# Attention's v product with seven block products from left sums in seven of its sixteen units, and v between k and q in two head groups

## The chip, the cores and the metric

One core of one Trainium2 chip runs the kernel, and one launch computes the whole network. The time is device microseconds of one execution; the median of three runs before the change is 2031.22 us (2029.69 to 2031.56). Engines are named as in the profile: PE (TensorE), ACT (ScalarE), DVE (VectorE), POOL (GpSimd) and SP (the engine that issues most DMAs).

## The reference: what is computed

A decoder of two layers on one sequence of 256 tokens with 2048 features, all in float32. Layer 0 is a pooling mixer and a gated FFN with a causal convolution of width 3; layer 1 is attention and another such FFN. What matters here is the attention:

```python
k_shared = (h @ shared_w_k).reshape(B_, S, N_HEADS, HEAD_DIM)
v_shared = (h @ shared_w_v).reshape(B_, S, N_HEADS, HEAD_DIM)
q = (h @ w_q).reshape(B_, S, N_HEADS, HEAD_DIM)
...
s = jnp.where(mask, s, NEG_INF)
m = jnp.max(s, axis=-1, keepdims=True)
pr = jnp.exp(s - m)
...
o = jnp.sum(wts[..., None] * jnp.stack(outs, axis=0), axis=0)
return o.reshape(B_, S, D_MODEL).astype(h.dtype) @ w_o
```

There are 16 heads of 128 features. With 256 tokens the three dilated branches come down to one softmax with a table of counts (`cnt`) and one of masks (`negm`).

## The kernel before

**Units.** The program is a list of units, and each unit multiplies one block of a weight matrix (512 rows by 512 columns) with the activations. `run_units` (L126) goes through the list: `ahead` (L111) issues the loads of the blocks up to five units ahead and splits the blocks up to three units ahead, then the unit's matmuls follow, then the pieces of work that `later(n, ...)` has put n units off, and last the evacuation of a group that is complete. A raw block has one of three buffers, a split block one of four.

**Split.** Every float32 operand is made of a high part and a low part (`wh` and `wl`, type fp32r). For a plain block ACT rounds the high part (L82) and DVE subtracts it (L83). A product of two such operands takes three matmuls: high by high, high by low, low by high.

**Two kinds of product.** `group` (L177) gives the result with features on the partitions. A pair there is one matmul of 512 columns, which does both halves of x at once (L165), and one of 256 (L166); a unit has 16 pairs. k and q are made in this way. `group_tm` (L189) gives it with tokens on the partitions: in `go_t` a unit is 24 matmuls of 512 columns (L238 to L240). All sixteen v units are of this kind before the change. `group_tm` has a second form, `mk_seven` (L202), used until now in the FFN's down projection alone. It treats tokens by features by columns as a product of 2 by 2 blocks and takes seven block products for eight (Strassen's scheme in Winograd's order), so that a unit has 7 x 2 x 3 = 42 matmuls of 256 columns (L227 to L229). It comes as two entries of the list, here called the a half (three products, 18 matmuls) and the b half (four products, 24 matmuls). Its block is split by `split_sums` (L90): for the a half ACT runs L103 twice and DVE L104, L106 twice, L107 and L109, for the b half ACT runs L96 twice and DVE L97 twice. It needs four sums of blocks of the left operand, each in high and low part.

**Attention.** The heads come in four head groups of four heads; they are numbered 0 to 3 here. Before the change each group runs four k units, four q units and four v units. What follows a group's q is put off by units: `scores` of heads 0 and 1 after two units and of heads 2 and 3 after three (PE L988 and L989, then a softmax of small steps on DVE and ACT, L994 to L1011). In groups 0 to 2 the probabilities are turned without PE: `blocks` (L1030) lets DVE transpose blocks of 32 by 32 for two heads at once (L1034, tile `pb`), and 16 DMAs on SP then move the blocks to their places (`move`, L1040 to L1043, tile `pTs`). This is done for heads 0 and 1 four units after q and for heads 2 and 3 seven units after q; the DMAs go in two lots of eight, one and two units later. Tile `pb` has one buffer, so the second transposition waits until the first 16 moves have landed. `outputs` (L1048) multiplies with v: heads 0 and 1 four units after v, heads 2 and 3 seven units after v (PE L1056 and L1057, then ACT L1058 and DVE L1059).

Each engine runs its own instructions in a fixed order, SP its DMAs too; an instruction whose inputs or buffers are not there yet holds up all that stand behind it on its engine.

## Time and profile before

| what | value |
|---|---|
| median of three runs (range) | 2031.22 us (2029.69 to 2031.56) |
| the profiled execution | 2031.27 us; its span 2029.5 us, 1.8 us lie around it |
| busy share: PE, weight load, DVE, ACT | 100%, 89%, 82%, 62% |
| chain that ended last | PE 99% |
| from head group 0's q to the end of head group 3's v | 953.1 to 1219.2 us of the span |
| granted PE clock over the span | 0.999 |

Times in the trace are microseconds from the span's start. "Busy" of PE counts a matmul from its start to a modelled end, and matmuls overlap in the pipeline: a matmul of 512 columns is shown with about 396 ns and one of 256 with about 281 ns. What a unit costs is therefore read from the distance between the starts of two units, not from these durations.

### The profile page before, as it was taken

To read this page: it belongs to the slowest core of one execution; us is meant where nothing else is said; L and a number is where in the kernel's file an instruction comes from. 1 tells how busy PE (TensorE), PEld (TensorE's weight loads), DVE (VectorE), ACT (ScalarE), POOL (GpSimd) and SP (SyncE) were. 2 spreads that over 40 slices of the span, in tenths; PEclk is the share of its full clock that TensorE was granted. 3 is DMA by queue.
4 is the path that set the end of the run, shared out by engine and by line. 5 is a ranking of instruction groups with operands and counts; after the bars stand their busy time and mean duration, and the time that the engine had idled before them with its cause. 6 is when DMAs were issued, how large, how long until landed. Compare 5 with 4: busy or idle time off the path is not lost.

```text
span 2029.5 us, 31025 instructions
## 1 busy us (share of the span) xinstructions
PE 2021.9 (100%) x12460; PEld 1807.1 (89%) x12460; DVE 1664.9 (82%) x1979; ACT 1253.3 (62%) x1676; POOL 75.0 (4%) x111
## 2 busy tenths in 40 slices
PE   9999999999999999999999999999999999999999
PEld 8898988899889988889888888998899989989987
DVE  6859887899789988879756657787889888989898
ACT  6544686667766675657533444577667676667672
POOL 2000000000000001100000000000000000100100
PEclk9999999999999999999999999999999999999999
DMA  8565467666655667864566555557666756666665
GB/s 258 203 206 189 164 208 208 192 191 227 207 193 188 229 206 206 229 221 166 193 197 192 169 185 171 187 177 218 187 197 198 228 187 212 198 214 197 208 213 180
DMA packets 278304, 405.90 MB, mean 200 GB/s; under 512 B 80414, under 2 KB 95668, under 8 KB 277904
## 3 DMA queue, kind: packets, MB, share of 16 engines
q1 hardware_dynamic: 266144, 389.72, 58.0%
q0 software_dynamic: 11584, 13.55, 4.4%
q8 instruction: 97, 1.59, 0.3%
q10 hardware_dynamic: 432, 0.66, 0.1%
q14 instruction: 47, 0.39, 0.1%
HBM read 380.01 MB, written 2.10 MB: 188 GB/s over the span
## 4 chain that ended last, share of the span: by engine, by line
PE 99%; DMA 0%; SPq 0%; DVE 0%; ACT 0%; issue 0%; DVEq 0%
PE acc L165 43%; PE acc L166 22%; PE t L238 3%; PE t L240 3%; PE t L239 3%; PE acc L169 3%; PE acc L170 3%; PE acc L168 3%; PE s L228 3%; PE s L227 2%; PE s L229 2%; PE t L228 2%; PE t L227 2%; PE t L229 2%; PE s L989 0%; PE o L1056 0%
## 5 line engine op out<-in xcount | busy, mean ns | idle before, releaser
L165 PE MATMUL acc<-xc,wh 128*128 128x512 f32 x3264 | 1151.9, 396 | 0.0
L166 PE MATMUL acc<-xc,wl 128*128 128x256 f32 x3264 | 915.9, 281 | 0.0
L83 DVE TENSOR_TENSOR wl<-raw,wh 128x2048 fp32r<-128x2048 f32 (+2 forms) x322 | 697.0, 2169 | 251.7 <-ACT wh L82 248.6
L165 PEld LDWEIGHTS acc<-xc,wh 128*128 128x128 f32 x3264 | 615.9, 189 | 144.0 <-DVE o L1059 0.6
L82 ACT CAST wh<-raw 128x2048 fp32r<-128x2048 f32 (+2 forms) x322 | 582.0, 1812 | 221.4 <-PE acc L165 120.3
L166 PEld LDWEIGHTS acc<-xc,wl 128*128 128x128 f32 x3264 | 615.4, 189 | 0.5
L96 ACT CAST wh<-raw 128x1024 fp32r<-128x1024 f32 x108 | 112.9, 1053 | 149.0 <-DVE raw L107 123.1
L97 DVE TENSOR_TENSOR wl<-raw,wh 128x1024 fp32r<-128x1024 f32 x108 | 129.1, 1221 | 1.4 <-ACT wh L96 1.4
L103 ACT CAST wh<-raw 128x1024 fp32r<-128x1024 f32 x108 | 84.5, 832 | 48.5 <-PE acc L165 33.8
L586 ACT ACTIVATE c<-u,cv 128x256 f32<-128x256 f32 x172 | 89.6, 594 | 18.7 <-DVE f L649 8.2
L106 DVE TENSOR_TENSOR wl<-raw,wh 128x1024 fp32r<-128x1024 f32 x108 | 98.3, 951 | 1.7 <-ACT wh L103 1.4
L228 PE MATMUL t<-wl,g 128*128 128x256 f32 x320 | 89.8, 281 | 0.0
L227 PE MATMUL t<-wh,g 128*128 128x256 f32 x320 | 89.8, 281 | 0.0
L229 PE MATMUL t<-wh,g 128*128 128x256 f32 x320 | 89.7, 280 | 0.0
L271 POOL DMA_DIRECT2D ht<-w x24 | 20.3, 847 | 1809.2 <-ACT wh L103 771.9
L577 ACT COPY u<-acc 128x256 f32<-128x256 f32 x164 | 54.7, 373 | 51.5 <-PE acc L166 51.4
L591 ACT ACTIVATE a<-u,cv 128x256 f32<-128x256 f32 x172 | 73.5, 500 | 12.3 <-DVE g L659 6.5
L229 PE MATMUL s<-wh,xs 128*128 128x256 f32 x284 | 79.2, 279 | 0.0
L228 PE MATMUL s<-wl,xs 128*128 128x256 f32 x284 | 79.2, 279 | 0.0
L227 PE MATMUL s<-wh,xs 128*128 128x256 f32 x284 | 79.2, 279 | 0.0
L591 ACT ACTIVATE u<-u,cv 128x256 f32<-128x256 f32 x172 | 73.5, 500 | 0.0
L238 PE MATMUL t<-wh,g 128*128 128x512 f32 (+1 forms) x179 | 68.2, 381 | 0.0
(279 smaller groups left out, 3439.2 us busy)
## 6 DMA issues: line engine op xcount, KB each, us to landing
raw<-in_ffn_w_up_dram SPq DMA_DIRECT2D x160, 1024.0 KB, 4.9
raw<-in_ffn_w_down_dram SPq DMA_DIRECT2D x80, 1024.0 KB, 5.1
raw<-in_pool_w_out_dram SPq DMA_DIRECT2D x16, 1024.0 KB, 5.0
raw<-in_shared_w_k_dram SPq DMA_DIRECT2D x16, 1024.0 KB, 5.0
raw<-in_attn_w_q_dram SPq DMA_DIRECT2D x16, 1024.0 KB, 5.3
raw<-in_shared_w_v_dram SPq DMA_DIRECT2D x16, 1024.0 KB, 5.9
raw<-in_attn_w_o_dram SPq DMA_DIRECT2D x16, 1024.0 KB, 5.0
raw<-in_pool_w_in_dram SPq DMA_DIRECT2D x12, 1024.0 KB, 5.4
```

The source lines that it names most:

```text
L82: A.copy(wh[i][:, s], r[:, s])
L83: V.tensor_tensor(wl[i][:, s], r[:, s], wh[i][:, s].bitcast(F32), OP.subtract)
L96: A.copy(h[:, :, n], r[:, :, n])
L97: V.tensor_tensor(l[:, :, n], r[:, :, n], h[:, :, n].bitcast(F32), OP.subtract)
L106: V.tensor_tensor(l[:, k, n], r[:, k, n], h[:, k, n].bitcast(F32), OP.subtract)
L165: PE.matmul(ps[m], h[:, k, c], q[:, k, :, :T], start=st, stop=False)
L166: PE.matmul(ps[m][:, :T], l[:, k, c], q[:, k, 0, :T], start=False, stop=sp and not shifted)
L227: PE.matmul(to, xh, h[:, k, n], start=opens and kk == 0, stop=False)
L228: PE.matmul(to, xh, l[:, k, n], start=False, stop=False)
L229: PE.matmul(to, xl, h[:, k, n], start=False, stop=ends and kk == 1)
L238: PE.matmul(to, xh, h[:, k, c], start=j == 0 and k == 0, stop=False)
L591: A.activation(to[:, m, :], u[:, m, i:i + T], AF.Copy, scale=cv[:, i, j:j + 1])
```

## The change

Seven of the sixteen v units take the form of `mk_seven`: in head groups 1 and 2 the blocks 1, 2 and 3 of the rows, in head group 3 block 3. In head groups 1 and 2 the v units now stand between the k units and the q units. The left sums of x are formed once, by `v_sums` (DVE additions on 128x256, then a split on ACT and DVE), four units after the q of head group 0; those of block 3 take five small tiles, those of blocks 1 and 2 one tile `xsum` each. v is evacuated by `v_early` (ACT copies, DVE adds; four of the products) and by additions in `v_post`, where a copy stood before. `outputs` of groups 0 to 2 are now put off from q instead of v, by eight and eleven units; `transposes` and `outputs` of group 3 are as before. An a half and a b half count as one unit each in these distances.

Of k, v and q in the head groups 1 and 2 the list now reads: four k units, one plain v unit, a and b halves of three v units, four q units. Lines move: scores L988 is now L1044, `blocks` L1034 is L1090, the moves L1043 are L1099, `outputs` L1056 and L1057 are L1112 and L1113, its copies L1059 are L1115, the evacuation of q and k L974 is L1026.

PE at the outputs of heads 0 and 1 of head group 1. In the kernel before they stand between the fourth k unit and the first q unit of head group 2 (each `wh` number is one weight block; `acc` is the result of k, then of q):

```order
L165 MATMUL acc<-xc,wh_10267 128x512
L166 MATMUL acc<-xc,wl_10268 128x256
L1056 MATMUL o<-pTs,vt 128x256
L1057 MATMUL o<-pTs,vt 128x128
L1056 MATMUL o<-pTs,vt 128x256
L1057 MATMUL o<-pTs,vt 128x128
L165 MATMUL acc<-xc,wh_10317 128x512
L166 MATMUL acc<-xc,wl_10318 128x256
```

In the changed kernel they stand between the a half and the b half of the second seven-product unit of head group 2's v (`t` and `s` are banks of the v product, `xsum` the left sums):

```order
L229 MATMUL t_10573<-wh_10564,xsum 128x256
L1112 MATMUL o<-pTs,vt 128x256
L1113 MATMUL o<-pTs,vt 128x128
L1112 MATMUL o<-pTs,vt 128x256
L1113 MATMUL o<-pTs,vt 128x128
L227 MATMUL s_10576<-wh_10609,xsum 128x256
L228 MATMUL s_10576<-wl_10610,xsum 128x256
```

In both kernels the fourth k unit and the transposition of heads 0 and 1 lie before these rows; what PE has between the transposition and the outputs was four units of k and is now one plain v unit, one a half, one b half and one a half. The outputs of heads 2 and 3 now follow the third b half.

DVE from the first transposition (`pb<-p`) of head group 1 to the second. Before the change:

```order
L83 TENSOR_TENSOR wl_10232<-raw_10107,wh_10231 128x2048
L1034 STREAM_TRANSPOSE pb<-p 128x768
L952 COPY vt<-t_10082 128x512
L83 TENSOR_TENSOR wl_10268<-raw_10168,wh_10267 128x2048
L83 TENSOR_TENSOR wl_10318<-raw_10229,wh_10317 128x2048
L83 TENSOR_TENSOR wl_10364<-raw_10265,wh_10363 128x2048
L1034 STREAM_TRANSPOSE pb<-p 128x768
```

In the changed kernel (`k<-k,acc` is the evacuation of k; two seven-product blocks, `raw_10438` and `raw_10562`, are split between the transpositions):

```order
L97 TENSOR_TENSOR wl_10513<-raw_10329,wh_10512 128x4x256 x2
L1090 STREAM_TRANSPOSE pb<-p 128x768
L1026 TENSOR_TENSOR k<-k,acc 128x256 x4
L104 TENSOR_TENSOR raw_10438<-raw_10438 128x2x256
L106 TENSOR_TENSOR wl_10565<-raw_10438,wh_10564 128x4x256
L106 TENSOR_TENSOR wl_10565<-raw_10438,wh_10564 128x2x256
L107 TENSOR_TENSOR raw_10438<-raw_10438 128x2x256
L109 TENSOR_TENSOR raw_10438<-raw_10438 128x4x256
L97 TENSOR_TENSOR wl_10610<-raw_10438,wh_10609 128x4x256 x2
...
L109 TENSOR_TENSOR raw_10562<-raw_10562 128x4x256
L1090 STREAM_TRANSPOSE pb<-p 128x768
L97 TENSOR_TENSOR wl_10682<-raw_10562,wh_10681 128x4x256 x2
```

The scores' steps and one seven-product split (a half, then b half) stand ahead of the first transposition here, where plain splits stood.

SP's queue at the same place in the changed kernel (`raw` is a load of a weight block, `pTs<-pb` a move):

```order
L72 DMA raw_10562<-in_shared_w_v_dram 128x4x512
L1099 DMA pTs<-pb 32x6x32 x16
L72 DMA raw_10641<-in_attn_w_q_dram 128x4x512
L72 DMA raw_10679<-in_attn_w_q_dram 128x4x512
L1099 DMA pTs<-pb 32x6x32 x8
L72 DMA raw_10724<-in_attn_w_q_dram 128x4x512
L1099 DMA pTs<-pb 32x6x32 x8
```

Before the change a load stood between the first eight moves and the second eight; now the sixteen follow each other, and the second sixteen have a load in their middle as before.

The diff:

```diff
--- before.py
+++ after.py
@@ -943,19 +943,71 @@
     scale = 1.0 / math.sqrt(P)
     qk, pr, oq, pT, vts = {}, {}, {}, {}, {}
 
+    def v_tile(c):
+        if c not in vts:
+            vts[c] = pools["attn"].tile([P, 2, 512], F32, name="vt", tag="vt")
+        return vts[c][:, 0, :], vts[c][:, 1, :]
+
     def v_post(c):
         def post(t, ps):
-            if t == 0:
-                vts[c] = pools["attn"].tile([P, 2, 512], F32, name="vt", tag="vt")
-                A.copy(vts[c][:, 0, :], ps)
+            v = v_tile(c)[t]
+            if c > 0:
+                V.tensor_tensor(v, v, ps, OP.add)
+            elif t == 0:
+                A.copy(v, ps)
             else:
-                V.tensor_copy(vts[c][:, 1, :], ps)
-                if c == 3:
-                    later(1, lambda: transposes(c, (0, 1)))
-                    later(2, lambda: transposes(c, (2, 3)))
-                later(2 if c == 3 else 4, lambda: outputs(c, (0, 1)))
-                later(3 if c == 3 else 7, lambda: outputs(c, (2, 3)))
+                V.tensor_copy(v, ps)
+            if t == 1 and c == 3:
+                later(1, lambda: transposes(c, (0, 1)))
+                later(2, lambda: transposes(c, (2, 3)))
+                later(2, lambda: outputs(c, (0, 1)))
+                later(3, lambda: outputs(c, (2, 3)))
         return post
+
+    def v_early(c):
+        def early(p16, p75):
+            v0, v1 = v_tile(c)
+            left, right = v0[:, :256], v0[:, 256:]
+            A.copy(left, p16[:, :256])
+            V.tensor_tensor(right, left, p16[:, 256:], OP.add)
+            V.tensor_tensor(v1[:, :256], right, p75[:, :256], OP.add)
+            V.tensor_tensor(right, right, p75[:, 256:], OP.add)
+            V.tensor_tensor(v1[:, 256:], v1[:, :256], p75[:, 256:], OP.add)
+        return early
+
+    vsums = {}
+
+    def v_sums(q, then):
+        ap = pools["attn"]
+        x = H[q]
+        a11, a12, a21, a22 = (x[:, k:k + 2, t * P:t * P + P] for k, t in ((0, 0), (2, 0), (0, 1), (2, 1)))
+        f = ap.tile([P, 4, T], F32, name="f", tag="k")
+        d = [f[:, i].rearrange("p (k t) -> p k t", k=2) for i in range(4)]
+        V.tensor_tensor(d[0], a21, a22, OP.add)
+        V.tensor_tensor(d[1], d[0], a11, OP.subtract)
+        V.tensor_tensor(d[2], a21, a11, OP.subtract)
+        V.tensor_tensor(d[3], a12, d[1], OP.subtract)
+
+        def rest():
+            if q < 3:
+                t = quad_tile("xsum")
+                vsums[q] = [[t[:, i, hl, :T].rearrange("p (k t) -> p k t", k=2) for hl in range(2)] for i in range(4)]
+                split_act(t, f)
+                then()
+                return
+            w = lnp.tile([P, 2, T], F32R, name="vs0", tag="fold2")
+            z = ap.tile([P, 2, T], F32R, name="vs3", tag="vs3")
+            vs = [[w[:, 0], w[:, 1]], [z[:, 0], z[:, 1]]]
+            for pair in (("S", "Q"), ("cs", "f1")):
+                vs.append([lnp.tile([P, T], F32R, name=f"vs{nm}", tag=nm) for nm in pair])
+            for i, v in enumerate(vs):
+                A.copy(v[0], f[:, i])
+            for i, v in enumerate(vs):
+                V.tensor_tensor(v[1], f[:, i], v[0].bitcast(F32), OP.subtract)
+            vsums[q] = [[u.rearrange("p (k t) -> p k t", k=2) for u in v] for v in vs]
+            then()
+
+        later(1, rest)
 
     def qk_post(nm, hq):
         def post(ps):
@@ -978,6 +1030,10 @@
                 if hq < 3:
                     later(4, lambda: blocks(hq, (0, 1)))
                     later(7, lambda: blocks(hq, (2, 3)))
+                    later(8, lambda: outputs(hq, (0, 1)))
+                    later(11, lambda: outputs(hq, (2, 3)))
+                if hq == 0:
+                    later(4, lambda: v_sums(3, lambda: v_sums(1, lambda: v_sums(2, lambda: None))))
         return post
 
     def scores(hq, ms):
@@ -1058,11 +1114,20 @@
             A.copy(oq[hq][:, m, 0, :T], ps[:, :T])
             V.tensor_tensor(oq[hq][:, m, 1, :T], ps[:, :T], oq[hq][:, m, 0, :T].bitcast(F32), OP.subtract)
 
+    def v_group(hq):
+        js = (0, 1, 2, 3)
+        seven = {0: (), 1: (1, 2, 3), 2: (1, 2, 3), 3: (3,)}[hq]
+        group_tm(shared_w_v, rows4, 512 * hq, 512, xsrcs, v_post(hq),
+                 seven={j: (lambda j=j: vsums[j]) for j in js if j in seven}, early=v_early(hq))
+
     for hq in range(4):
         x0 = hq == 0
         group(shared_w_k, rows4, 512 * hq, 512, psrcs if x0 else xsrcs, qk_post("k", hq), mode="x" if x0 else "ab")
+        if hq in (1, 2):
+            v_group(hq)
         group(attn_w_q[0], rows4, 512 * hq, 512, xsrcs, qk_post("q", hq))
-        group_tm(shared_w_v, rows4, 512 * hq, 512, xsrcs, v_post(hq))
+        if hq in (0, 3):
+            v_group(hq)
     add_last(attn_w_o[0], rows4, [lambda j=j: oq[j] for j in range(4)], True, 1, 0, after=to_tokens)
     marks.append(len(units))
     ffn(1)
```

## The prediction

> **What bounds the kernel now.** I read the page first: the shares of the engines, then the chain that ended last.
>
> ```profile
> PE 2021.9 (100%) x12460; PEld 1807.1 (89%) x12460; DVE 1664.9 (82%) x1979; ACT 1253.3 (62%) x1676; POOL 75.0 (4%) x111
> PE 99%; DMA 0%; SPq 0%; DVE 0%; ACT 0%; issue 0%; DVEq 0%
> ```
>
> PE never rests and makes up 99% of the chain, so a matmul less is time less, as long as nothing makes PE wait; and each wait that the change brings to PE is lost in full. Two questions follow: what seven products save per unit, and whether the cover of everything that runs beside v is still there.
>
> Next, the stages by windows. The rows are: two plain v units of head group 1 (48 matmuls; the counts include those that reach over an edge), two seven-product units of the FFN (84 matmuls), four k units, one pair of outputs, and the whole of group 1's v with both pairs of scores.
>
> ```profile
> 1048.70:1059.85 11.15, 11.15 (x51) 9.02 (x49) 5.03 (x4) 4.09 (x3) 0.00 (x0) 1.00 0.54 190
> 1841.35:1851.27 9.92, 9.92 (x86) 9.92 (x85) 8.60 (x12) 9.66 (x14) 0.00 (x0) 1.00 0.35 120
> 1073.64:1096.16 22.52, 22.52 (x129) 19.65 (x128) 13.85 (x9) 8.04 (x6) 0.00 (x0) 1.00 0.66 197
> 1096.16:1097.39 1.23, 1.23 (x11) 1.13 (x9) 0.00 (x0) 0.37 (x1) 0.00 (x0) 1.00 1.21 260
> 1048.70:1073.64 24.94, 24.94 (x114) 20.45 (x113) 17.41 (x49) 10.90 (x14) 0.00 (x0) 1.00 0.49 169
> ```
>
> A plain v unit takes 11.15 / 2 = 5.58 us, a seven-product unit 9.92 / 2 = 4.96, a k or q unit 22.52 / 4 = 5.63, a pair of outputs 1.23, both pairs of scores 24.94 - 4 x 5.58 = 2.64. Of the 4.96 the a half has 18 of 42 matmuls, 2.13 us, the b half 2.83.
>
> **The change: what PE saves.** Seven units go from 5.58 to 4.96: 7 x 0.62 = **-4.3 us**. The rows of the order leave no doubt that the matmuls go away.
>
> **What DVE gets.** The rows by form, for a plain block and then for the pieces of a seven-product block:
>
> ```profile
> L83 DVE TENSOR_TENSOR wl<-raw,wh 128x2048 fp32r<-128x2048 f32 x282 | 645.0, 2289 | 238.2 <-ACT wh L82 235.3 <-DMA pTs<-pb 2.0 <-PE vT L1128 0.4
> L97 DVE TENSOR_TENSOR wl<-raw,wh 128x1024 fp32r<-128x1024 f32 x108 | 129.1, 1221 | 1.4 <-ACT wh L96 1.4
> L109 DVE TENSOR_TENSOR raw<-raw 128x1024 f32<-128x1024 f32 x54 | 66.2, 1225 | 1.8
> L106 DVE TENSOR_TENSOR wl<-raw,wh 128x1024 fp32r<-128x1024 f32 x54 | 65.8, 1219 | 1.7 <-ACT wh L103 1.4
> L107 DVE TENSOR_TENSOR raw<-raw 128x512 f32<-128x512 f32 x54 | 37.4, 692 | 1.9
> L104 DVE TENSOR_TENSOR raw<-raw 128x512 f32<-128x512 f32 x54 | 36.9, 684 | 0.0
> L106 DVE TENSOR_TENSOR wl<-raw,wh 128x512 fp32r<-128x512 f32 x54 | 36.9, 683 | 0.0
> ```
>
> The a half costs DVE 0.68 + 1.22 + 0.68 + 0.69 + 1.23 = 4.50 us and the b half 2 x 1.22 = 2.44, so 6.94 against 2.29 for a plain block, and against 4.96 on PE. Alone this is no wait: splits run three units ahead. But it moves what stands behind them on DVE.
>
> **What covers the moves.** For head group 1, in order of time: the first score on DVE, the first transposition, SP's two lots of eight moves, the second transposition with its wait, its two lots, and the first outputs. After them the transposition pairs of groups 0 and 2.
>
> ```profile
> 1060.70 0.56 DVE L994 SCALAR_TENSOR_TENSOR p<-s,negm 128x384 f32<-128x384 f32 x1 [1.98 <-PE s L989]
> 1075.89 0.97 DVE L1034 STREAM_TRANSPOSE pb<-p 128x768 f32<-128x768 f32 x1
> 1076.94 5.14 SPq L1043 DMA_DIRECT2D pTs<-pb  x8
> 1082.77 6.56 SPq L1043 DMA_DIRECT2D pTs<-pb  x8
> 1091.01 0.98 DVE L1034 STREAM_TRANSPOSE pb<-p 128x768 f32<-128x768 f32 x1 [1.78 <-DMA pTs<-pb]
> 1092.05 6.17 SPq L1043 DMA_DIRECT2D pTs<-pb  x8
> 1098.90 5.55 SPq L1043 DMA_DIRECT2D pTs<-pb  x8
> 1096.16 0.59 PE L1056 MATMUL o<-pTs,vt 128*128 128x256 f32 x2
> ```
>
> ```profile
> 1003.12 0.97 DVE L1034 STREAM_TRANSPOSE pb<-p 128x768 f32<-128x768 f32 x1
> 1018.05 0.98 DVE L1034 STREAM_TRANSPOSE pb<-p 128x768 f32<-128x768 f32 x1 [1.59 <-DMA pTs<-pb]
> 1148.66 0.97 DVE L1034 STREAM_TRANSPOSE pb<-p 128x768 f32<-128x768 f32 x1
> 1163.05 0.98 DVE L1034 STREAM_TRANSPOSE pb<-p 128x768 f32<-128x768 f32 x1 [1.05 <-DMA pTs<-pb]
> ```
>
> The second transposition waits for the landing of the first 16 moves, so its start dates that landing: 15.12, 14.93 and 14.39 us after the first one. SP alone spends 0.64 us on each move. Before the change the outputs came 1096.16 - 1091.01 = 5.15 us after the landing; that is the whole margin.
>
> **Head group 2's v** (moves of group 1), with K the start of its k units. Before, the first transposition came 1075.89 - 1048.70 = 27.19 us after the start of the four units that hold the scores; those are now k units. Two units before the scores cost 11.26 for 11.15, and DVE's row has an a half for a plain split (4.50 for 2.29) and a b half for another (2.44 for 2.29): T0 = K + 27.19 + 0.11 + 2.21 + 0.15 = K + 29.66. PE reaches the outputs of heads 0 and 1 after four k units, scores, a plain v unit and halves a, b, a: 22.52 + 2.64 + 5.58 + 2.13 + 2.83 + 2.13 = K + 37.83. That leaves 8.2 us for what took 14.4 to 15.1. The load between the two lots is gone; with both lots at 5.14, 0.1 between them, 1.05 from the transposition to the first move and 1091.01 - 1089.33 = 1.68 from SP's last to the landing it is 13.1 us, so K + 42.8. **First wait: 4.9 us** (6.9 at 15.1).
>
> The second transposition stands on DVE behind the first one (0.97), four evacuations of k (0.41 each, row below) and halves a, b, a: T0 + 0.97 + 1.66 + 4.50 + 2.44 + 4.50 = K + 43.7. Its moves land 1.05 + 5.14 + 0.1 + 0.65 (a load) + 5.14 + 1.68 = 13.75 later, K + 57.5. PE, released at K + 42.8, does the outputs, b, a, b (1.23 + 2.83 + 2.13 + 2.83 = 9.02) and is there at K + 51.8. **Second wait: 5.7 us**. Lower end: without the 0.8 us in which consecutive DVE instructions overlap, 4.9. Upper end: moves as slow as group 0's second lots (SP's rows below: 1026.39 + 5.90 + 1.68 - 1018.05 = 15.9 us for 13.75) and the first wait at 6.9, which gives 6.9. Together 10.6 us, from 9.8 to 13.8.
>
> ```profile
> 1019.09 6.61 SPq L1043 DMA_DIRECT2D pTs<-pb  x8
> 1026.39 5.90 SPq L1043 DMA_DIRECT2D pTs<-pb  x8
> ```
>
> ```profile
> L974 DVE TENSOR_TENSOR k<-k,acc 128x256 f32<-128x256 f32 x12 | 4.2, 413 | 0.0
> L646 DVE TENSOR_TENSOR f<-f,c 128x256 f32<-128x256 f32 x16 | 6.8, 426 | 0.5
> L286 DVE TENSOR_TENSOR xc<-h,xc 128x1024 fp32r<-128x1024 f32 x12 | 14.6, 1219 | 0.0
> L952 DVE COPY vt<-t 128x512 f32<-128x512 f32 x4 | 2.6, 660 | 0.0
> ```
>
> **Head group 1's v** (moves of group 0). Here the first transposition stays where it was, 1075.89 - 1073.64 = 2.25 us after the end E of the v units, and the first outputs keep their four k units. Before the second transposition DVE now has the left sums: 12 additions and four low parts on 128x256 (16 x 0.43), a low part of 128x1024 (1.22), the copy 0.66, two plain splits (4.58), one a half (4.50) and the transposition's 0.97: E + 2.25 + 18.8 = E + 21.1; landing E + 34.8. PE: 22.52 + 1.23 + 5.58 + 4.96 = E + 34.3. The wait is **0.5 us**, from 0 to 2.7 by the slower moves. The other left-sum work is hidden: PE has the splits of the next three units by then.
>
> **Small terms.** The first q unit after group 2's second outputs takes banks that DVE must first copy out (L1115), behind the split of a q block whose load SP issues after eight of the moves: **0.5 us** (0 to 1.5). In group 3 the transposes on PE take banks that the new additions of v read, some 1.5 us of DVE behind two splits: **0.5 us** (0 to 1.5). `v_early` elsewhere, 4 x 0.42 + 2 x 0.66 us of DVE, hides under the q units. Head group 2's moves keep four units as cover: nothing.
>
> **The clock.** A wait of 5 us does one more thing. At the span's start the trace shows a stretch with gaps, what followed, and the longest gap in it:
>
> ```profile
> 4.58:11.41 6.83, 4.33 (x31) 3.67 (x31) 3.88 (x6) 3.55 (x6) 0.00 (x0) 1.00 0.85 271
> 11.41:14.82 3.41, 3.41 (x18) 3.41 (x17) 1.45 (x3) 1.81 (x4) 0.00 (x0) 0.50 1.05 401
> 9.53 0.38 PE L168 MATMUL acc<-xc,wh 128*128 128x256 f32 x1 [1.34 <-ACT wh L82]
> ```
>
> PE was busy 4.33 of 6.83 us, its longest gap was 1.34, and for the next 3.41 us the granted clock was 0.50: 1.7 us of work lost. After the first wait such a loss disappears in the second, which ends by the moves and not by PE; after the second it is paid: **1.7 us** (0 to 3.4).
>
> The Trainium skill, "TensorE: Matmul & The Clock Gate", Part 1, What's actually happening, sets another condition: the clock drops after a free-running window of about 3.4 us that is idle as a whole. By that rule the gap at the start would have cost nothing, where the row shows the drop; and of a 5.7 us wait about two in three would hold such a window (an estimate from the window that the Trainium skill gives there), so the term would be 1.7 or 0. By the skill's rule the sum is 2040.8 or 2039.1; by the row it is 2040.8.
>
> **Sum.** -4.3 + 10.6 + 0.5 + 0.5 + 0.5 + 1.7 = +9.5 us, or between -4.3 + 9.8 = +5.5 and -4.3 + 13.8 + 2.7 + 1.5 + 1.5 + 3.4 = +18.6. The profiled execution took 2031.27 us (span 2029.5 and 1.8 around it), 0.05 above the median, which I leave out: **2040.8 us**. A measurement tells about 0.2%, 4.1 us, from no change.
>
> **Rivals.**
> - *The cover holds* (2031.3 - 4.3 = **2027.0**, faster). It needs the moves to land within 8.2 us of the transposition, or the transposition 5 us earlier. For it: 5.15 us of margin, and no wait of PE anywhere now. Against it: 16 moves at 0.64 are 10.3 us of SP by themselves, and the scores ahead of the transposition wait for PE. 4%.
> - *One wait instead of two* (about **2033**, no change): if the second transposition came some 5 us earlier than DVE's row lets it, only the first wait would stay, -4.3 + 4.9 + 1.5 = +2.1. 8%.
> - *No drop of the clock* (**2039.1**): both waits as above without the 1.7. For it: each wait is a single gap with PE dense on both sides. 25%. This is also what the rule of the Trainium skill above (TensorE: Matmul & The Clock Gate, Part 1) gives for a wait that holds no whole window.
> - *DVE is late itself* (about **2047**, slower): three seven-product blocks in a row are 20.8 us of DVE for 14.9 on PE, a deficit of 5.9 in each of two groups; one such deficit on top of the sum is 2046.7. It decides where the lead of three units is used up before the b half of the third block. For it: DVE has left sums, scores and evacuations in the same stretch. Against it: while PE waits for the moves, DVE catches up, and the FFN window above ran two such units with DVE at 8.60 of 9.92 and no gap on PE. 14%.
> - The forecast, 49%.
>
> That the change isn't what it says I leave out: the order shows the matmuls and the waits' places.
>
> **From cases to numbers.** Slower by over 0.2% are the forecast, the case without the drop and late DVE: 0.88. Within 0.2%: 0.08. Faster: 0.04. The range runs from 2034 (the low end of the sum less some of the single-wait case) to 2047, where late DVE begins; it leaves out about 0.18.
>
> **What would show it.** Two seven-product units in 9.9 us; 16 moves on SP in a row of about 10.3 us; in head group 2, PE idle of some 5 us before the outputs twice, put down to the DMAs of `pTs`, and hardly any in head group 1; second transposition about 14 us after the first; a stretch of clock 0.50 after the last wait. The prediction is wrong if PE reaches the outputs with the moves landed, or if splits of DVE appear as what PE waits for.

## The result, and the profile after

| kernel | median of the runs | range |
|---|---|---|
| before | 2030.78 us | 2029.69 to 2031.96 |
| after | 2040.11 us | 2039.12 to 2041.01 |

The change makes the kernel slower by 9.3 us: ratio 1.0048, interval 1.0038 to 1.0059. The forecast was 2040.8. The profiled execution of the changed kernel took 2039.12 us, with a span of 2037.0 and a mean clock of 0.997; that is 7.9 us more than the profiled execution of the kernel before. One run of an experiment below, the order alone, took 4941.43 us and is left out of its ratio.

The page of the changed kernel, its engine shares and its chain:

```profile
PE 2023.3 (99%) x12586; PEld 1814.8 (89%) x12586; DVE 1707.3 (84%) x2054; ACT 1267.9 (62%) x1703; POOL 75.0 (4%) x111
PE 97%; DMA 1%; DVE 1%; SPq 1%; issue 0%; ACT 0%; DVEq 0%; ACTq 0%
```

PE falls from 99% to 97% of the chain, and DMA, DVE and SP's queue come in. PE's busy time did not fall by 4 us, although there is less work: part of the work ran at half clock.

Now the stages of the changed kernel, by windows (length, then busy time and instruction count of PE, weight load, DVE, ACT and POOL, then the clock, the DMA share and GB/s). The rows are: head group 1's v with both pairs of outputs, two seven-product units in it, head group 2's v with both pairs of outputs, and the six units of q and k behind it up to the first scores.

```profile
1022.64:1045.78 23.14, 23.14 (x168) 21.85 (x167) 21.37 (x26) 13.62 (x19) 0.00 (x0) 1.00 0.70 215
1035.75:1045.78 10.03, 10.03 (x87) 10.03 (x86) 8.77 (x8) 6.37 (x7) 0.00 (x0) 1.00 0.86 309
1093.45:1127.63 34.18, 26.74 (x168) 24.75 (x167) 27.12 (x37) 17.01 (x21) 0.00 (x0) 0.89 0.46 129
1127.63:1162.65 35.02, 35.02 (x195) 30.54 (x194) 19.20 (x19) 13.38 (x12) 0.00 (x0) 0.96 0.65 228
```

Both v stages hold the same work: 2 x 1.23 + 5.58 + 3 x 4.96 = 22.92 us by the prediction's rows. Head group 1 takes 0.2 more, head group 2 takes 11.3 more, and the six units behind it 35.02 - 6 x 5.63 = 1.2 more.

Three views show where the 11.3 go. DVE's two transpositions for head group 1's heads, the moves in SP's queue behind them (the loads between them are left out), and PE's two starts of outputs, with the idle time ahead of each in brackets:

```profile
1097.57 0.97 DVE L1090 STREAM_TRANSPOSE pb<-p 128x768 f32<-128x768 f32 x1
1110.73 0.97 DVE L1090 STREAM_TRANSPOSE pb<-p 128x768 f32<-128x768 f32 x1
```

```profile
1098.61 10.33 SPq L1099 DMA_DIRECT2D pTs<-pb  x16
1111.77 6.18 SPq L1099 DMA_DIRECT2D pTs<-pb  x8
1118.63 5.95 SPq L1099 DMA_DIRECT2D pTs<-pb  x8
```

```profile
1110.54 1.19 PE L1112 MATMUL o<-pTs,vt 128*128 128x256 f32 x2 [4.23 <-DMA pTs<-pb]
1125.94 0.67 PE L1112 MATMUL o<-pTs,vt 128*128 128x256 f32 x2 [3.21 <-DMA pTs<-pb]
```

SP issues the last of the first sixteen moves at 1108.94, and PE starts 1.6 us later; it issues the last of the second sixteen at 1124.58, and PE starts 1.4 us later. PE's idle time is 4.2 and 3.2, 7.4 together, not 11.3. The clock has most of the rest. The rows are the 3.41 us before each drop of the clock and the stretch at 0.50 behind it:

```profile
1106.36:1109.77 3.41, 0.00 (x0) 0.00 (x0) 3.34 (x6) 0.45 (x2) 0.00 (x0) 1.00 0.28 42
1109.77:1116.60 6.83, 6.06 (x24) 5.73 (x25) 5.15 (x7) 4.63 (x5) 0.00 (x0) 0.50 0.93 318
1123.42:1126.84 3.42, 0.90 (x5) 0.88 (x6) 0.83 (x1) 1.90 (x1) 0.00 (x0) 1.00 0.32 66
1126.84:1130.25 3.41, 3.41 (x12) 2.87 (x12) 3.34 (x7) 1.25 (x4) 0.00 (x0) 0.50 1.04 402
```

The clock falls to 0.50 at 1109.77, while PE still waits, and stays there for 6.83 us. PE works through 6.06 of them, so it comes to the second outputs about 3 us late and waits that much less there. Seen from PE's program, the second wait is the one that counts: it ends when SP's moves end, whatever PE did before.

### The profile page after: what moved, and what is told of

Its sections match the earlier page's. It is cut to its first block, busy times and chain, and to the rows that moved or that the text cites. A ratio compares the mean times of both kernels' runs of the same rounds, so it can differ in the third digit from the quotient of the medians.

```text
span 2037.0 us, 31392 instructions
## 1 busy us (share of the span) xinstructions
PE 2023.3 (99%) x12586; PEld 1814.8 (89%) x12586; DVE 1707.3 (84%) x2054; ACT 1267.9 (62%) x1703; POOL 75.0 (4%) x111
## 4 chain that ended last, share of the span: by engine, by line
PE 97%; DMA 1%; DVE 1%; SPq 1%; issue 0%; ACT 0%; DVEq 0%; ACTq 0%
PE acc L165 43%; PE acc L166 22%; PE acc L169 3%; PE acc L168 3%; PE acc L170 3%; PE t L238 3%; PE t L240 3%; PE t L239 3%; PE s L227 3%; PE s L228 3%; PE s L229 3%; PE t L228 2%; PE t L227 2%; PE t L229 2%; DMA raw<-in_attn_w_q_dram 1%; SPq L1099 0%
## 5 line engine op out<-in xcount | busy, mean ns | idle before, releaser
L83 DVE TENSOR_TENSOR wl<-raw,wh 128x2048 fp32r<-128x2048 f32 (+2 forms) x315 | 680.6, 2166 | 233.4 <-ACT wh L82 229.5
L82 ACT CAST wh<-raw 128x2048 fp32r<-128x2048 f32 (+2 forms) x315 | 568.5, 1810 | 208.4 <-PE acc L165 116.7
L96 ACT CAST wh<-raw 128x1024 fp32r<-128x1024 f32 x122 | 127.3, 1052 | 165.3 <-DVE raw L107 133.5
L97 DVE TENSOR_TENSOR wl<-raw,wh 128x1024 fp32r<-128x1024 f32 x122 | 145.6, 1221 | 1.7 <-ACT wh L96 1.7
L103 ACT CAST wh<-raw 128x1024 fp32r<-128x1024 f32 x122 | 95.6, 834 | 48.5 <-PE acc L165 33.5
L106 DVE TENSOR_TENSOR wl<-raw,wh 128x1024 fp32r<-128x1024 f32 x122 | 111.0, 951 | 2.2 <-ACT wh L103 2.0
L109 DVE TENSOR_TENSOR raw<-raw 128x1024 f32<-128x1024 f32 x61 | 74.7, 1225 | 2.1
```

The costliest lines, as they stand in the source:

```text
L82: A.copy(wh[i][:, s], r[:, s])
L83: V.tensor_tensor(wl[i][:, s], r[:, s], wh[i][:, s].bitcast(F32), OP.subtract)
L96: A.copy(h[:, :, n], r[:, :, n])
L97: V.tensor_tensor(l[:, :, n], r[:, :, n], h[:, :, n].bitcast(F32), OP.subtract)
L103: A.copy(h[:, k, n], r[:, k, n])
L106: V.tensor_tensor(l[:, k, n], r[:, k, n], h[:, k, n].bitcast(F32), OP.subtract)
```

## The experiments

All ratios and differences are to the kernel before, with runs of both on the same chip. On this scale the changed kernel stands at +9.3 us, 1.0048 (1.0038 to 1.0059). The medians of the kernel before differ between these chips by up to 1.2 us, so two kernels are compared by their differences.

| kernel | median us | difference, us | ratio (interval) | expected us |
|---|---|---|---|---|
| cover cut in the kernel before | 2037.44 | +7.1 | 1.0035 (1.0023 to 1.0048) | 2038.6 |
| order alone | 2037.31 | +7.0 | 1.0032 (1.0020 to 1.0044) | 2030.8 |
| filler in the waits | 2038.94 | +8.6 | 1.0041 (1.0027 to 1.0054) | 2038.9 |
| half of the moves on POOL | 2038.38 | +8.1 | 1.0037 (1.0025 to 1.0050) | 2033.0 |
| wide moves | 2037.86 | +7.8 | 1.0037 (1.0025 to 1.0050) | 2037.0 |
| early transpositions | 2043.89 | +13.8 | 1.0068 (1.0056 to 1.0081) | 2037.6 |
| wide and early | 2044.51 | +14.5 | 1.0066 (1.0053 to 1.0078) | 2031.6 |
| wide, early, POOL | 2037.06 | +7.1 | 1.0034 (1.0021 to 1.0048) | 2027.5, or 2032 to 2038 |
| head group 2 in the old order | 2027.71 | -2.4 | 0.9989 (0.9980 to 0.9998) | 2028 to 2030 |
| PE transposes in head group 1 | 2033.44 | +3.5 | 1.0015 (1.0007 to 1.0024) | 2027.6 |
| the same, outputs one entry earlier | 2028.57 | -2.6 | 0.9989 (0.9980 to 0.9998) | 2028.3 |
| six units, two of them in head group 2 | 2032.83 | +2.9 | 1.0014 (1.0006 to 1.0023) | 2027.1 |

The theory was that head group 1's moves no longer fit under head group 2's v units, and that each such wait is followed by a stretch at half clock. The rivals were late splits on DVE, the order itself, and a clock that does not drop.

### Cover against moves, without any of the change

```diff
-                later(2 if c == 3 else 4, lambda: outputs(c, (0, 1)))
+                later(2 if c in (1, 3) else 4, lambda: outputs(c, (0, 1)))
```

> The kernel before, with one number changed: the outputs of heads 0 and 1 of head group 1 come two units after v instead of four. No seven-product units and no left sums. Their cover becomes 2 x 5.63 = 11.26 us shorter, against the margin of 5.15 us between the landing and the outputs. Theory (cover against moves decides, by the difference): one wait of PE of 11.26 - 5.15 = 6.1 us, put down to the DMAs of pTs, then a stretch at clock 0.50 that costs about 1.7: 2030.8 + 7.8 = 2038.6 us. Rival 1 (the clock does not drop after a single clean gap with PE dense on both sides): 2036.9. Rival 2 (the moves are not what holds PE): 2030.8.

It took 7.1 us more than before. PE's wait, then windows of the wait and of the 3.41 us behind it:

```profile
1089.06 1.19 PE L1056 MATMUL o<-pTs,vt 128*128 128x256 f32 x2 [5.17 <-DMA pTs<-pb]
```

```profile
1083.89:1089.06 5.17, 0.00 (x0) 0.03 (x1) 0.00 (x0) 0.00 (x0) 0.00 (x0) 0.98 0.67 185
1089.06:1092.47 3.41, 3.41 (x11) 2.94 (x12) 0.49 (x2) 0.85 (x3) 0.00 (x0) 0.54 0.83 299
```

The clock fell at 1088.80, in the last 0.26 us of the wait, for 3.41 us. One wait of 5.17 us and half of the 3.15 us that PE then worked at half clock make 6.7 of the 7.1. The wait is 0.9 shorter than the expected 6.1 because the moves landed 14.3 us after their transposition (1074.8) instead of 15.1. So cover against moves decides, with no seven-product unit in sight. And the rival that a single clean gap costs no clock falls here: PE was dense on both sides of this one.

### The order alone

The changed kernel with `seven = ()` and the plain evacuation of v, without left sums; v stays between k and q in head groups 1 and 2.

```diff
-        seven = {0: (), 1: (1, 2, 3), 2: (1, 2, 3), 3: (3,)}[hq]
+        seven = ()
...
-            if c > 0:
-                V.tensor_tensor(v, v, ps, OP.add)
-            elif t == 0:
+            if t == 0:
...
-                if hq == 0:
-                    later(4, lambda: v_sums(3, lambda: v_sums(1, lambda: v_sums(2, lambda: None))))
```

> The new order alone: v between k and q in head groups 1 and 2, outputs put off from q by eight and eleven units, all sixteen v units plain, no left sums. This tells whether the place of v costs anything by itself. Theory (the waits come from cover that is counted in units, and a seven-product block counts as two of them while it takes 4.96 us of PE; with plain units the cover in time is what it was, and DVE has no seven-product splits ahead of the transpositions): no new wait, 2030.8 us, within 1 us. Rival (the order itself takes the cover away, since the scores now have v units and not k units behind them, or k units ahead): waits of some us in head group 2, 2033 to 2040.

A miss: 7 us slower. But the reason is neither theory. ACT at the end of head group 2's v, then PE at the q units behind it:

```profile
1136.26 0.59 ACT L955 COPY vt<-t 128x512 f32<-128x512 f32 x1 [17.81 <-PE o L1109]
1136.74 5.51 ACT L82 CAST wh<-raw 128x2048 fp32r<-128x2048 f32 x3
```

```profile
1138.70 0.79 PE L165 MATMUL acc<-xc,wh 128*128 128x512 f32 x1 [2.47 <-ACT wh L82]
1141.03 0.58 PE L166 MATMUL acc<-xc,wl 128*128 128x256 f32 x1 [1.53 <-DVE wl L83]
```

Tile `vt` has one buffer. With four plain entries the v group ends before the outputs of heads 2 and 3, eleven entries after q, have read the old `vt`; so ACT's copy of the new v waits 17.8 us for them, and all splits stand behind it. In the changed kernel v has seven entries, and the outputs come first. This run therefore doesn't tell what the place of v alone costs; a run with a second `vt`, which could tell, was not made. It does show that PE never waited for the moves of head group 1 here: with plain units in the same order the cover still held.

### Filler: does idleness make the clock drop?

```diff
             t = pT.pop((hq, m))
+            if hq == 1 and m % 2 == 0:
+                for _ in range(34 if m == 0 else 52):
+                    PE.matmul(ps[:, :T], neg1, XC[0][:, 0, 0, :T], start=True, stop=True)
```

> The changed kernel with filler matmuls of 128x256 (0.118 us each by the seven-product units' pace, 4.96 / 42) ahead of head group 1's outputs: 34 ahead of heads 0 and 1 (4.0 us) and 52 ahead of heads 2 and 3 (6.1 us). They write the outputs' bank, which the outputs then overwrite, so what is computed stays. PE should reach the first outputs at 1106.13 + 4.0 = 1110.1, just before they were released in the changed kernel (1110.54), and the second ones at about 1110.5 + 1.23 + 7.8 + 6.1 = 1125.7, just before 1125.94. Theory (PE waits for the moves, and the idle time makes the clock drop): both outputs start where they did, within 0.5 us, no stretch at clock 0.50 is left there, and the q units behind them lose their 1.24 us: 2040.1 - 1.2 = 2038.9 us. Rival 1 (the clock drops whatever PE does, or because of what runs beside it): 2040.1, with the same two stretches at 0.50. Rival 2 (PE is late through its own work): the filler is paid in full, 2040.1 + 10 = 2050.

PE's starts of the second outputs and of a matmul of the first q unit that waits for a bank, then the windows from the first outputs on, and of the q and k units:

```profile
1126.77 0.70 PE L1115 MATMUL o<-pTs,vt 128*128 128x256 f32 x2 [1.10 <-DMA pTs<-pb]
1129.57 0.50 PE L165 MATMUL acc<-xc,wh 128*128 128x512 f32 x1 [0.53 <-DVE o L1118]
```

```profile
1110.14:1126.77 16.63, 15.53 (x127) 15.22 (x127) 8.65 (x8) 7.45 (x7) 0.00 (x0) 1.00 0.72 213
1128.10:1162.73 34.63, 34.10 (x195) 29.54 (x194) 19.62 (x19) 13.39 (x12) 0.00 (x0) 1.00 0.71 237
```

The clock stays at 1.00 throughout, so it is PE's idleness that made it drop, not what runs beside. Behind ten microseconds of filler PE still waited 1.10 us for the moves: it had that time to spare. The median is the expected one, but that is in part luck. The second outputs came 33.8 us after the start of the stage (1093.00) instead of 32.5: the first eight of the second sixteen moves held SP for 7.60 us, where it was 6.18 in the changed kernel. The spans of the two profiled executions are 2037.2 and 2037.0, and the interval overlaps that of the changed kernel. The q units still take 34.63: without the drop a wait at a bank (0.53) shows that the drop had covered. So the drop after the second wait was worth some 0.4 net here (35.02 - 34.63), not 1.7.

### Half of the moves on POOL

```diff
-                    nc.sync.dma_start(to[32 * j:32 * j + 32, i], fr[32 * i:32 * i + 32, j])
+                    (nc.sync if j < 2 or hq != 1 else nc.gpsimd).dma_start(to[32 * j:32 * j + 32, i], fr[32 * i:32 * i + 32, j])
```

> The changed kernel with half of head group 1's moves (j = 2 and 3) issued by POOL instead of SP. Theory (the moves' issue on SP sets both landings): if POOL issues at SP's pace, the first sixteen land 1.05 + 5.2 + 1.7 = 8.0 us after their transposition, which is 1105.5 against PE's 1106.1, so the first wait goes; the second transposition stays where DVE lets it (13.2 us after the first), its moves land 8.6 us later (1119.3) against PE's 1115.2, so one wait of about 4.2 us is left of 11.3: 2040.1 - 7.1 = 2033.0 us (some 1.2 less if the clock then does not drop). If POOL's issue is slower than SP's (up to 1.0 us each), the landings come 3 us later: about 2037. Rival (DVE's splits, not the moves, hold PE): second wait as before, gain 0 to 2 us, 2038 to 2040.

A miss: it stands 8.1 us above the kernel before, with an interval that overlaps that of the changed kernel, where a gain of 7.1 was expected. The first wait went, as expected: PE came to the first outputs and went on. The second did not shrink to 4.2 but grew to 7.65. SP's queue behind the second transposition, POOL's last issues, PE's wait, and the window between the last issue and the landing:

```profile
1111.91 2.54 SPq L1099 DMA_DIRECT2D pTs<-pb  x4
1114.56 0.91 SPq L72 DMA_DIRECT2D raw<-in_attn_w_q_dram  x1
1115.51 2.59 SPq L1099 DMA_DIRECT2D pTs<-pb  x4
```

```profile
1113.72 3.96 POOL L1099 DMA_DIRECT2D pTs<-pb  x7 [0.55 <-issue]
```

```profile
1123.65 1.19 PE L1112 MATMUL o<-pTs,vt 128*128 128x256 f32 x2 [7.65 <-DMA pTs<-pb]
```

```profile
1118.10:1123.65 5.55, 0.00 (x1) 0.04 (x1) 1.87 (x2) 1.90 (x1) 0.00 (x0) 0.56 1.11 309
```

All moves are issued by 1118.1, 6.5 us sooner than in the changed kernel, yet they land at 1123.65, 5.5 us later instead of 1.4, and so only 2.3 us sooner than there. In that time the DMA engines are full (share 1.11) with weight blocks of 1 MB each, whose loads SP issued in between. So shorter issue let the moves meet the loads; that the loads are what delays them is read from these rows and was not tried by itself. The Trainium skill, "DMA: Bandwidth & Descriptors", Issuing engines are not separate DMA queues, says that another issuing engine saves only the time of issue, which it calls usually small, and that all transfers interleave on the same 16 DMA engines. The second half fits these rows; "usually small" does not fit the changed kernel, where SP's issue was 10.33 us of the 13.0 from the first transposition to PE's start.

### What a move costs, and when it starts

Three kernels. The first changes the layout so that a move takes 32 pieces of 768 bytes instead of 192 of 128:

```diff
-        V.transpose(b, two.rearrange("p h s k -> p (h s k)"))
+        V.transpose(b.rearrange("p (b k j) -> p k b j", b=4, k=6), two.rearrange("p h s (b j) -> p (h s) b j", b=4))
...
-        to = t.rearrange("p h s -> p (h s)").rearrange("p (k a j) -> p a k j", k=6, a=4)
-        fr = b.rearrange("p (k b j) -> p b k j", k=6, b=4)
+        to = t.rearrange("p h s -> p (h s)").rearrange("p (a x) -> p a x", a=4)
+        fr = b.rearrange("p (b x) -> p b x", b=4)
+        for m in ms:
+            pT[hq, m] = to.rearrange("p a (h s j) -> p h s a j", h=2, s=3)[:, m % 2]
...
-            PE.matmul(ps[:, :T], vt[:, 0, hd], t[:, :T], start=True, stop=False)
-            PE.matmul(ps[:, P:T], vt[:, 1, hd], t[:, T:], start=False, stop=True)
+            lo, hi = (t[:, :T], t[:, T:]) if hq == 3 else (t[:, :2], t[:, 2])
+            PE.matmul(ps[:, :T], vt[:, 0, hd], lo, start=True, stop=False)
+            PE.matmul(ps[:, P:T], vt[:, 1, hd], hi, start=False, stop=True)
```

> The changed kernel with another layout of the turned probabilities: each of the 16 moves takes 32 pieces of 768 bytes instead of 192 pieces of 128, the same bytes; DVE's transposition writes its blocks in that order and the outputs read pTs with a stride. It tells what sets SP's 0.6 us of a move. Theory (part of it is the number of pieces): a move has 192 pieces and takes 0.604 in the queue's rows, a weight load of 512 pieces 0.91, so by that slope 32 pieces would take 0.45, 16 moves 7.2 instead of 10.3, and both landings come 3.1 earlier. The second transposition stays where DVE lets it, so the second landing decides: 2040.1 - 3.1 = 2037.0 us. Rival (a move costs the same whatever its pieces): 2040.1. If the stride costs PE or DVE something: above 2040.

SP's queue with these moves:

```profile
1098.18 10.02 SPq L1101 DMA_DIRECT2D pTs<-pb  x16
```

Sixteen moves take 10.02 instead of 10.33: on SP a move costs nearly the same 0.6 us with 32 pieces as with 192. On the price of a move the rival was right. The time, 7.8 us above the kernel before where the changed kernel is 9.3 above, lies between the two expectations; the intervals overlap, and what the rest of the difference is was not looked into.

The second issues head group 1's transpositions one unit earlier:

```diff
-                    later(4, lambda: blocks(hq, (0, 1)))
-                    later(7, lambda: blocks(hq, (2, 3)))
+                    later(3 if hq == 1 else 4, lambda: blocks(hq, (0, 1)))
+                    later(6 if hq == 1 else 7, lambda: blocks(hq, (2, 3)))
```

> The changed kernel with head group 1's transpositions one unit earlier (three and six units after q instead of four and seven); moves go with them, outputs stay. The first one then stands ahead of a b half's split on DVE (2.4 us), the second ahead of an a half's (4.5 us), but tile pb has one buffer, so the second waits for the first landing. Theory (the second landing ends the chain; it follows the second transposition, which follows DVE's splits): first transposition at 1097.6 - 2.4 = 1095.2, first landing at about 1108.2, second transposition there instead of 1110.7, so the second landing comes 2.5 earlier: 2040.1 - 2.5 = 2037.6 us. Rival (DVE's splits, which the transposition now pushes back, hold PE): 2040 or more.

It is 13.8 us above the kernel before, so 4.5 slower than the changed kernel instead of 2.5 faster. The outputs did come earlier by some 1.5 us against the start of the stage, but PE then met a wait that no step of mine had at that size. SP, ACT and PE behind the second outputs (which started at 1125.35), and the six units:

```profile
1117.24 6.70 SPq L1099 DMA_DIRECT2D pTs<-pb  x8
1124.04 1.09 SPq L72 DMA_DIRECT2D raw<-in_attn_w_q_dram  x2
```

```profile
1129.30 1.90 ACT L82 CAST wh<-raw 128x2048 fp32r<-128x2048 f32 x1 [3.96 <-DMA raw<-in_attn_w_q_dram]
1131.11 0.64 ACT L1114 CAST o<-o 128x256 fp32r<-128x256 f32 x2
```

```profile
1133.91 0.79 PE L165 MATMUL acc<-xc,wh 128*128 128x512 f32 x1 [4.39 <-DVE o L1115]
```

```profile
1127.90:1169.70 41.80, 37.41 (x195) 32.16 (x195) 20.73 (x19) 15.38 (x14) 0.00 (x0) 0.90 0.61 207
```

The moves now stand ahead of one more q block on SP. That block lands at 1129.3, ACT splits it and only then makes the copy of the outputs (L1114), DVE does the same (L1115), and PE waits 4.39 us for the bank that this copy frees. The six units take 41.80, 8.0 more than they need: that wait, and two stretches at half clock.

The first wait of this kernel shows something else. PE's row, and a window of 6.83 us around the wait:

```profile
1110.42 0.67 PE L1112 MATMUL o<-pTs,vt 128*128 128x256 f32 x2 [3.21 <-DMA pTs<-pb]
```

```profile
1105.66:1112.49 6.83, 3.62 (x28) 3.35 (x27) 3.87 (x5) 2.07 (x3) 0.00 (x0) 1.00 0.73 205
```

It is as long as the second wait of the changed kernel, 3.21 us, but the clock stays at 1.00. So not every such wait is followed by a stretch at half clock. A clock that is set by fixed windows of 3.41 us would fit: counted back from the later drops, a border between two windows lies inside this wait (1.86 and 1.35 us), while 2.51 of the other 3.21 lay in one window. That was not tried by itself, and it leaves open how much work in a window is enough: at the start of the kernel before PE was busy for 1.85 of the 3.41 us ahead of a drop (8.00 to 11.41), and here for 1.56 in one of the two windows, without one.

The third has both edits:

> Both of these edits together: wide moves and transpositions one unit earlier. Theory: first transposition 1095.2, its moves land 10 us later (1105.2), before PE's 1106.1; the second transposition then no longer waits for them but for DVE's splits (1106.2), and its moves land 10.7 to 12 us later, 1117 to 1118, against PE's 1115.2: one wait of 2 to 3 us is left of 11.3, so 2040.1 - 8.5 = 2031.6 us, up to 1 less if the clock then does not drop. If the wide moves are no faster: first landing 1108.2, as in the early kernel, 2037.6. Rival (loads of weights on the same DMA engines, not SP's queue, date the landing): 2035 to 2038.

A miss of 13 us: PE waited 4.5 us at the same bank, and the clock was at 0.50 for 13.65 us there.

And with half of the moves on POOL as well:

> The changed kernel with wide moves, head group 1's transpositions one unit earlier, and half of its moves on POOL. Theory 1 (with two queues the moves fit the cover): first landing 1.05 + 5.0 + 1.7 after 1095.3, 1103, before PE (1106.1) and before DVE is free for the second transposition (1106.2); its moves land 8 us later, 1114.2, before PE's 1115.2; no wait is left, 2030.1 - 4.3 + 1.5 = 2027.5 us. Theory 2 (the moves share SP's queue and the DMA engines with the weight loads, which the two earlier runs showed: landings 5.5 us after the last issue with POOL, and 5 us of PE at the banks behind a late q block with early transpositions): the second landing comes at 1118 or later and the q units lose some us, 2032 to 2038.

PE's two starts of outputs and its wait behind them:

```profile
1108.08 0.67 PE L1115 MATMUL o<-pTs,vt 128*128 128x256 f32 x2 [0.45 <-DMA pTs<-pb]
1118.89 0.67 PE L1115 MATMUL o<-pTs,vt 128*128 128x256 f32 x2 [1.42 <-DMA pTs<-pb]
1126.79 0.80 PE L165 MATMUL acc<-xc,wh 128*128 128x512 f32 x1 [5.64 <-DVE o L1118]
```

Here the two waits for moves shrank to 0.45 and 1.42 us, the best of these kernels, and theory 2 held: PE waited 5.64 us for DVE L1118, the copy that frees the bank, and the six units took 41.9. So what was gained at the outputs was given back right behind them.

### Head group 2 in the old order

```diff
-        seven = {0: (), 1: (1, 2, 3), 2: (1, 2, 3), 3: (3,)}[hq]
+        seven = {0: (), 1: (1, 2, 3), 2: (3,), 3: (3,)}[hq]
...
-        if hq in (1, 2):
+        if hq == 1:
             v_group(hq)
...
-        if hq in (0, 3):
+        if hq != 1:
             v_group(hq)
```

> The changed kernel with head group 2 back in the old order (k, q, v) and only its block 3 in seven products: five seven-product units in place of seven, v between k and q in head group 1 alone, the left sums as before. Theory (all of the loss arises in head group 2, where halves of a seven-product unit are the cover of group 1's moves): the two waits go; saving 5 x 0.62 = 3.1, against 0.2 in head group 1 and 0.5 in head group 3, and in group 2 up to 2 because the outputs, put off by eight units from q, now have one b half (2.83) for a k unit (5.63) in their cover of 5.15 us of margin: 2030.3 - 3.1 + 0.7 + 0 to 2 = 2028 to 2030 us. Rival (the left sums, the new evacuation or v ahead of q in itself cost time): 2033 or more.

It is faster than the kernel before, by 2.4 us (2030.06 on the same chip). Its chain, from its page:

```profile
PE 99%; DMA 0%; SPq 0%; issue 0%; ACT 0%; DVE 0%; DVEq 0%
```

PE is 99% of it again. Of the 3.1 us that five units should save, 2.4 arrive. So the left sums, the new evacuation and v ahead of q in head group 1 cost little, and the loss belongs to head group 2.

### PE transposes: the moves taken away

```diff
-                    later(4, lambda: blocks(hq, (0, 1)))
-                    later(7, lambda: blocks(hq, (2, 3)))
+                    turn = transposes if hq == 1 else blocks
+                    later(6 if hq == 1 else 4, lambda: turn(hq, (0, 1)))
+                    later(8 if hq == 1 else 7, lambda: turn(hq, (2, 3)))
```

> The changed kernel with head group 1's probabilities turned by PE (transposes, as in head group 3), six and eight units after q, instead of by DVE and 32 moves; seven seven-product units, order and outputs as in the changed kernel. Theory (the moves are the whole loss): both waits and the half-clock stretches go, SP's queue is free for the loads. PE pays 12 transposes, 2 x 0.57 by head group 3's row of before. 2030.1 - 4.3 + 1.1 + 0.2 (head group 1) + 0.5 (head group 3) = 2027.6 us, up to 1 more for waits at banks. Rival (DVE's splits in head group 2's v are late in any case): PE waits for wl there, 2033 or more.

It ends 3.5 us above the kernel before where the changed kernel ends 9.3 above, a gain of about 6, and PE has no wait for the outputs. What is left does not come from a late `wl`. ACT, DVE and PE behind the second outputs (1117.60 to 1118.83), and windows of the 3.41 us behind the wait and of the six units:

```profile
1118.45 1.91 ACT L82 CAST wh<-raw 128x2048 fp32r<-128x2048 f32 x1 [1.48 <-PE o L1114]
1120.26 0.63 ACT L1115 CAST o<-o 128x256 fp32r<-128x256 f32 x2
```

```profile
1120.39 2.29 DVE L83 TENSOR_TENSOR wl<-raw,wh 128x2048 fp32r<-128x2048 f32 x1 [0.69 <-ACT wh L82]
1122.60 0.75 DVE L1116 TENSOR_TENSOR o<-o 128x256 fp32r<-128x256 f32 x2
```

```profile
1123.07 0.51 PE L165 MATMUL acc<-xc,wh 128*128 128x512 f32 x1 [3.28 <-DVE o L1116]
```

```profile
1123.07:1126.48 3.41, 3.41 (x12) 2.87 (x13) 3.34 (x8) 1.44 (x1) 0.00 (x0) 0.58 1.04 389
1118.83:1157.75 38.92, 35.64 (x195) 30.79 (x194) 21.59 (x20) 15.07 (x14) 0.00 (x0) 0.96 0.63 216
```

ACT holds a split of 1.91 us that can start only when PE is at the outputs, and the copy of the outputs stands behind it; DVE holds the low part of the same block, 2.29 us, ahead of its own copy. Together they are the time from the outputs to 1122.6, while PE has four matmuls to do before it needs the bank. The clock was at 0.50 for 3.41 us from 1123.62 on. The wait of 3.28 and half of these 3.41 make 5.0 of the 5.1 by which these units exceed 33.78.

### The same with the outputs one entry earlier

```diff
-                    later(11, lambda: outputs(hq, (2, 3)))
+                    later(10 if hq == 1 else 11, lambda: outputs(hq, (2, 3)))
```

> The kernel with PE transposes in head group 1, and its outputs of heads 2 and 3 one entry earlier (ten after q instead of eleven): they then stand ahead of the third b half, and their copies on ACT and DVE ahead of the split of one more q block. In the kernel with PE transposes PE had no wait for moves, but 3.28 us in the first q unit of head group 2, put down to DVE L1116 (the copy that frees a bank of the outputs), and a stretch at half clock behind it; those q units took 38.92 against 33.78. Theory (the copy stands behind splits of q blocks in ACT's and DVE's order; once it is ahead of one, a b half of 2.83 us on PE hides it): that wait and the half clock go, 2033.4 - 5.1 = 2028.3 us, within 1. Rival (DVE and ACT are short of time for the splits themselves, so that the wait moves to the splits of the q units): 2031 to 2034.

It did what was expected of it: 2028.57, where the kernel before took 2031.21 on the same chip. DVE's copy, PE's wait and the six units:

```profile
1118.03 0.75 DVE L1116 TENSOR_TENSOR o<-o 128x256 fp32r<-128x256 f32 x2
```

```profile
1118.50 0.51 PE L165 MATMUL acc<-xc,wh 128*128 128x512 f32 x1 [0.39 <-DVE o L1116]
```

```profile
1117.26:1151.66 34.40, 34.01 (x194) 29.46 (x193) 21.46 (x20) 14.46 (x12) 0.00 (x0) 1.00 0.70 244
```

The copy begins 0.8 us after the q units' start (1117.26) instead of 3.8 (1118.83 there), the wait is 0.39, the clock stays at 1.00, and the six units take 34.40 instead of 38.92. This kernel has all seven seven-product units in the changed order. It and the kernel with head group 2 in the old order beat both the kernel before and the changed one.

### Six units

The edit is against the kernel with head group 2 in the old order and five units: there blocks 1 and 3 take the form of seven products, and the outputs come ten and thirteen entries after q.

```diff
-        seven = {0: (), 1: (1, 2, 3), 2: (3,), 3: (3,)}[hq]
+        seven = {0: (), 1: (1, 2, 3), 2: (1, 3), 3: (3,)}[hq]
...
-                    later(8, lambda: outputs(hq, (0, 1)))
-                    later(11, lambda: outputs(hq, (2, 3)))
+                    later(10 if hq == 2 else 8, lambda: outputs(hq, (0, 1)))
+                    later(13 if hq == 2 else 11, lambda: outputs(hq, (2, 3)))
```

> Head group 1 as in the changed kernel, head group 2 in the old order with its blocks 1 and 3 in seven products (six seven-product units in all), and its outputs put off by ten and thirteen units from q. Theory (away from the moves each seven-product unit is worth its 0.62): 0.6 below the kernel with five, 2027.7 - 0.6 = 2027.1 us, no wait of PE for moves. Rival (the second seven-product block in head group 2 brings a wait through DVE or the moves): 2027.7 or more.

A miss: 5 us above the kernel with five. PE behind head group 2's first outputs, which now stand ahead of head group 3's first q unit, and a window from the first of these q units to the second outputs:

```profile
1172.32 0.79 PE L165 MATMUL acc<-xc,wh 128*128 128x512 f32 x1 [2.81 <-DVE o L1115]
```

```profile
1168.56:1191.40 22.84, 20.03 (x99) 17.13 (x98) 11.15 (x10) 8.41 (x10) 0.00 (x0) 0.85 0.73 241
```

It is the wait at a bank again, in another place, and a stretch of 6.83 us at half clock comes with it: the three units of this window take 22.84 instead of 3 x 5.63 = 16.89. Whether the second seven-product block or the new place of the outputs brings it was not separated.

## Why the prediction was right, point by point

- **What PE saves.** Two units took 10.03, so a unit is worth 5.58 - 5.01 = 0.57 and the seven 4.0, for 4.3.
- **Head group 2.** Lost 11.3 against 10.6. With the measured start of the k units at K = 1068.3 (1045.78 and four q units of 5.63), the first transposition came at K + 29.3 (predicted 29.66), PE's first outputs at K + 42.2 (42.8) and the second ones at K + 57.6 (57.5). That the last one fits so well is luck: its parts missed in opposite directions. The second transposition was 1.3 earlier (K + 42.4 for 43.7), and its moves took 15.2 us instead of 13.75, as the prediction's upper bound had it (15.9).
- **Head group 1.** Lost 0.2 for 0.5. **Head group 3** lost 0.4 for 0.5: from the end of its v to its last outputs 21.06 us (1226.03 to 1247.09) instead of 20.69 (1219.18 to 1239.87), with 0.4 put down to the transposes' wait for the additions of v (DVE L975). The terms add up to -4.0 + 11.3 + 0.2 + 0.4 + 1.2 = 9.1, where the medians differ by 9.3 and the two profiled executions by 7.9, so the last microsecond of this sum is not settled.
- **The clock and q's banks.** 1.7 + 0.5 predicted, 1.2 measured in the six units behind. The drop came with both waits, as the prediction said, and the first was hidden in the second; it was 6.83 long, not 3.41. The rule of the Trainium skill that the prediction weighed ("TensorE: Matmul & The Clock Gate", Part 1, What's actually happening) wants a whole idle window of about 3.4 us. The first wait agrees with it: PE was idle through the 3.41 us before the drop at 1109.77. The second does not: it was 3.21 us long, too short for such a window, and PE was busy for 0.90 of the 3.42 us before the drop at 1126.84; nor does the gap of 3.28 us in the kernel with PE transposes. That this term was paid is in part luck too, since the wait of 3.21 us in the kernel with early transpositions brought no drop.
- **The rivals.** The cover did not hold, there were two waits, and the clock dropped. DVE was not late with splits: in the changed kernel PE never waits for a `wl` in these stages.

One step was right only in its sum. I costed **q's banks** at 0.5 (0 to 1.5). That holds while PE waits for the moves, since ACT then makes its split (1124.08 to 1125.98) inside PE's wait, and PE, at half clock, reaches the bank only at 1129.06, when DVE's copy (1128.22 to 1128.97) is done. With the moves out of the way the same step costs 3.3 of wait and 1.7 of clock (38.92 for 33.78), and up to 8 where SP brings the q blocks late. So the moves' 11.3 were never all to be had by curing the moves: PE transposes gave about 6, and another 6 came only when the copies were put ahead of a split. Two waits lay one under the other, and the prediction had priced the lower one by what was left to see of it.

## What to carry to other kernels

Count cover in microseconds, not in entries of a list: when a unit is cut into two entries, everything that is put off by entries comes due sooner. Before a wait is taken away, look what else comes due within its length; ACT, DVE and SP catch up in it, and their own lateness shows only when it is gone. A short copy that frees a bank belongs ahead of the long splits in an engine's order, and an experiment that moves one number (outputs at ten instead of eleven) can tell this from a lack of time.

## What the runs showed of the hardware

- On SP a small move costs about 0.6 us of issue, with 192 pieces or with 32: 10.33 us for 16 of the one kind, 10.02 for 16 of the other. POOL issued seven in 3.96.
- The clock fell to 0.50 with gaps of PE of 5.17, 4.23, 3.28, 3.21, 2.81 (six units) and 2.47 us (order alone), and not with one of 3.21 in the kernel with early transpositions. With filler in the gaps it stayed at 1.00.
- Within these kernels a stretch at 0.50 lasted 3.41 us or a multiple of it: 6.83 in the changed kernel, 10.24 with half of the moves on POOL, 13.65 with wide moves and early transpositions. In the changed kernel PE was busy for 2.64 us of the first 3.41 and for all of the second.
- Moves that were issued 6.5 us sooner landed only 2.3 us sooner with 1 MB loads under way: 5.5 us from the last issue to the landing at a DMA share of 1.11, against 1.4 to 1.6 in the changed kernel.
